# Four units instead of three go feature tile by feature tile at the start of a two-layer trunk

## The chip, the cores and the metric

The kernel runs on one core of a Trainium2 chip. The metric is the device time of one execution in microseconds (us). TensorE multiplies, VectorE (DVE) and ScalarE (ACT) read its results out of PSUM and work on them, GpSimd (POOL) helps with element-wise work, and SyncE (SP) issues the transfers (DMA) between HBM and the on-chip memory SBUF.

## What is computed

Two layers of a transformer trunk work on 640 tokens of 1024 features: 512 latent tokens and 128 context tokens. Cut to what matters here:

```python
def layer(x, cond, lp, layer_idx, ctx_cache):
    mod = silu(cond) @ lp["w_ada"] + lp["b_ada"]          # 6 * 1024 columns
    sh1, sc1, g1, sh2, sc2, g2 = split(mod, 6)
    y, new_ctx = mixers(x * (1.0 + sc1) + sh1, lp, ...)   # the input h of the projection
    x = layer_norm(ALPHA * x + g1 * y, ...)
    ...
def mixers(h, lp, lam, lam_init, ctx_cache):
    a_x, a_b, a_c, d_q, d_k, d_v, m_cq, m_ckv, m_kpe = split(h @ lp["w_in"])
    y_a = a_b * short_conv(a_c * a_x, lp["conv_w"])
    ...                                                   # differential attention on d_*, latent attention on m_*
```

The first layer can't start its projection h @ w_in before the columns sh1 and sc1 of mod are there, which takes 8.4 MB of w_ada.

## The kernel before

Features lie on the 128 partitions, tokens in the free dimension: h is 8 feature tiles (NK = 8) of 128 x 640, each held as a rounded part and a remainder (hi, lo), and so is every weight tile. One product is three matmuls: hi by hi, hi by lo, lo by hi. The 640 tokens are split into region A (columns 0 to 384) and region B (384 to 640), since one PSUM bank holds 512 columns. A unit is 128 output columns of w_in: 8 feature tiles x 2 regions x 3 = 48 matmuls. The units come in the order of WIN: ax0, ac0, ab0, ax1, dk0, dq0, dk1, dq1, dv, and so on. ax, ac and ab belong to the short convolution, dk and dq to the differential attention. dv has another shape (dv_job).

Startup. setup issues, on SP's one queue, w_ada in five groups (FIRST: feature tile 0, then 1 and 2, 3 and 4, 5 and 6, 7), after each group the x of its feature tiles, and then weight tiles of w_in up to the count in PUMP. ada_first multiplies a group of w_ada on TensorE (L461), transposes the sums (L468), and modulate makes h of these feature tiles (L631, L638, L639). jobs3 holds the matmuls of the first three units (L386), feature tile by feature tile, so that they can go on while later groups arrive. Each of the three has a PSUM tile of its own. The units after that go through job and matmul3 (L343), one unit after the other, region A for all feature tiles and then region B.

Weights. A weight tile arrives in one of three staging buffers (stg), ScalarE casts it to hi (L142) and VectorE subtracts to get lo (L144) into one of four buffers (wu). W.get hands out the next unit, W.done gives its buffer back, and pump starts what has become possible.

PSUM. In the stage "any", mm() hands out three tiles of two banks each in turn. From dq1 on (SCORE_AT) the stage is "score": two tiles and one for scores, in the same six banks. A tile is free again when what it held has been read: in_evac does that for each unit, ax by a copy on ScalarE (L854), ac by three products on VectorE (L865, L866, L868), ab by products on VectorE that read PSUM at the end of the convolution (L884 to L888), dk and dq by ScalarE (L905, L906, L918, L919).

After each unit that doesn't go through jobs3, self.ada(ADA_IN) adds one step of the modulation that later stages need: 16 small matmuls (L434) on tiles rawt of w_ada, an addition on VectorE (L497), and after four steps a transpose (L441). During dv the first scores (L1192) of the differential attention are made, from dqp and dkp, which dq0 and dk0 reach through HBM (ddq, ddk).

The order of the instructions on each engine is set when the program is built, by a planner that simulates the timeline; an edge (issue_after, the helper behind) can force one instruction behind another. On the chip each engine works through its list in that order.

Of the kernel before, what the change touches and what calls it, by code (L numbers as in the profile page):

```python
# [18 lines left out]
NK = 8  # L19
# [8 lines left out]
SKEW = 4  # L28
# [18 lines left out]
SPLIT_POOL = ("y3", "y4", "y7")  # L47
W_POOL = False
FIRST = ((0, 1), (1, 2), (3, 2), (5, 2), (7, 1))
PUMP = (3, 3, 3, 3, 4, 4)  # L50
MODV = True
PIN = 3
TABLE = True
# [41 lines left out]
REG = {"A": (0, 384), "B": (384, 640)}  # L95
# [97 lines left out]
class Trunk:  # L193
# [181 lines left out]
    def window(self, hooks):  # L375
        self.nhook, self.hooks, self.urgent = 0, hooks, None

    def jobs3(self, us, x):

        nc = self.nc  # L380
        out = [self.mm()[:, 128:768] for _ in us]
        for k in range(NK):
            for u, ps in zip(us, out):
                for c0, c1 in REG.values():
                    for i, (pw, px) in enumerate(((0, 0), (0, 1), (1, 0))):
                        nc.tensor.matmul(ps[:, c0:c1], u[:, pw, 128 * k:128 * k + 128], x(k, px)[:, c0:c1],  # L386
                                         start=(k == 0 and i == 0), stop=(k == NK - 1 and i == 2))
        return out


# [456 lines left out]
    def in_evac(self, l, n, ps, regs):  # L847
        nc = self.nc
        if n in ("ax0", "ax1"):
            if "B" in regs:  # L850
                self.ax = self.t(name="ax")
                self.axs[n] = self.ax
            c0, c1 = (0, T) if regs == "AB" else REG[regs]
            nc.scalar.copy(self.axs[n][:, c0:c1], ps[:, c0:c1])  # L854
        elif n in ("ac0", "ac1"):
            m = n[-1]
            if "B" in regs:
                u = self.t(name="upad", n=644)
                self.us[m] = u
                nc.vector.memset(u[:, 0:1], 0.0)  # L860
                nc.vector.memset(u[:, 513:515], 0.0)
                nc.vector.memset(u[:, 643:644], 0.0)
            u, ax = self.us[m], self.axs["ax" + m]
            if "A" in regs:
                nc.vector.tensor_mul(u[:, 1:257], ps[:, 0:256], ax[:, 0:256])  # L865
                nc.vector.tensor_mul(u[:, 515:643], ps[:, 256:384], ax[:, 256:384])  # L866
            if "B" in regs:
                nc.vector.tensor_mul(u[:, 257:513], ps[:, 384:640], ax[:, 384:640])  # L868
        elif n in ("ab0", "ab1"):
            m = int(n[-1])  # L870
            u = self.us[n[-1]]
            if "B" in regs:
                self.ys[m] = self.t(name="y")
                self.abt = self.t(name="abt")
            if regs != "AB":
                c0, c1 = REG[regs]
                nc.scalar.copy(self.abt[:, c0:c1], ps[:, c0:c1])
                if regs == "B":
                    return
                ps = self.abt  # L880
            y = self.ys[m]
            w = [self.col("conv_w", l, 2 * i + m) for i in range(3)]
            cv = self.t(name="cv", n=642)
            nc.gpsimd.tensor_scalar(cv, u[:, 0:642], w[0], 0.0, ALU.mult, ALU.add)  # L884
            nc.vector.scalar_tensor_tensor(cv, u[:, 1:643], w[1], cv, ALU.mult, ALU.add)
            nc.vector.scalar_tensor_tensor(cv, u[:, 2:644], w[2], cv, ALU.mult, ALU.add)
            nc.vector.tensor_mul(lat(y), lat(ps), two(cv[:, 0:512]))
            nc.vector.tensor_mul(y[:, 256:384], ps[:, 256:384], cv[:, 514:642])  # L888
            nc.sync.dma_start(self.yd[m], self.ys.pop(m))
        elif n[:3] == "ckv" or n[:2] == "cq":  # L890
            raw, sq = self.t(name="raw"), self.t(name="sqr")
            nc.scalar.copy(raw, ps)
            nc.scalar.activation(sq, raw, AF.Square)
            rows = self.raws.setdefault(n[:-1], [])
            if rows:
                (nc.vector if n in ("ckv1", "cq2") else nc.gpsimd).tensor_add(sq, sq, rows[-1][1])
            rows.append((raw, sq))
            if n == "ckv1":
                self.norm_ckv(l)
            elif n == "cq2":  # L900
                self.norm_cq(l)
        elif n[:2] == "dk":
            m = int(n[-1])
            src = self.t(name="dk")
            nc.scalar.copy(src, ps)  # L905
            nc.scalar.copy(self.kp32[:, m, :], ps[:, 256:384])  # L906
            self.rope_lat(src, nc.vector if "k" in ROPE_V else nc.gpsimd)
            nc.vector.tensor_copy(src[:, 256:384], self.ckT[:, m, :])

            def rest():  # L910
                self.dkh[m] = self.split(src, "dk")

            self.soon(DEFER[2], rest)
            nc.sync.dma_start(self.o["state_diff_k"][l, m], self.kp32[:, m, :])
        elif n[:2] == "dq":
            m = int(n[-1])
            src = self.t(name="dq")
            nc.scalar.activation(src, ps, AF.Copy, scale=DIFF_SCALE)  # L918
            nc.scalar.copy(self.qp32[:, m, :], src[:, 256:384])  # L919
            self.rope_lat(src, nc.vector if "q" in ROPE_V else nc.gpsimd)  # L920

            def rest():
                qh, ql = self.split_q(src, "dq")
                kh, kl = self.dkh.pop(m)
                for i, (q, k) in enumerate(((qh, kh), (qh, kl), (ql, kh))):
                    self.move(self.ddq[m][:, i, :], q)
                    self.move(self.ddk[m][:, i, :], k)
                if m == 0:
                    self.assemble_diff(0)

            self.soon(DEFER[2], rest)
# [104 lines left out]
    def stage_in(self, l):  # L1036
        nc, a = self.nc, self.a
# [17 lines left out]

        names = [n for n, _ in WIN]
        h = lambda k, p: self.h[k][p]
        nskew = SKEW if l else 3
        if not l:
            us = [self.W.get((n, l)) for n in names[:nskew]]  # L1060
            for n, ps in zip(names, self.jobs3(us, h)):
                self.W.done()
                self.in_evac(l, n, ps, "AB")
                self.tick()
        else:
            us = [self.W.get((n, l)) for n in names[:nskew]]
            for regs in "BA":
                if regs == "B":
                    self.window(NEXT_IN)
                for i in range(0, nskew, 2):  # L1070
                    for n, ps in zip(names[i:i + 2], self.jobs2(us[i:i + 2], h, regs, NK)):
                        self.in_evac(l, n, ps, regs)
                        if regs == "A":
                            self.W.done()
                            self.tick()
                self.ln_inputs()
            self.ln_outputs(0 if OUTR else 1 << 30)
        for n in names[nskew:]:
# [4 lines left out]
            else:  # L1083
                u = self.W.get((n, l))
                mid, end = STEPS.get(n, (0, 0))
# [625 lines left out]
```

## Time and profile before

| | us |
|---|---|
| median of 3 runs | 1777.19 |
| lowest and highest | 1774.91, 1778.72 |
| profiled execution | 1775.88 |
| its span, first to last instruction | 1774.1 |
| TensorE busy in the span | 1702.8 |

The profiled execution is one of its own, 1.31 us below the median. Its span leaves out what lies before the first and behind the last instruction, 1.8 us. In the profile, PE is TensorE's matmuls and PEld its weight loads, which overlap them; a matmul's end is modelled, so that bars of neighbouring matmuls overlap, and the distance of two starts says more than a bar's length. Times are counted from the start of the span.

### The profile page before, as it was taken

Reading aid. Unit: us, or ns where it says so; the run is one execution under the profiler, and the core shown is the slowest. Engines: PE = TensorE matmul, PEld = TensorE weight load, DVE = VectorE, ACT = ScalarE, POOL = GpSimd, SP = SyncE. Lnnn points to the kernel's source line nnn. Section 1 sums busy time; section 2 is a strip of 40 time slices with the busy share of each in tenths; the row PEclk is TensorE's granted clock in tenths of the full one; section 3 lists DMA queues with packets and bytes.
Section 4 is the critical chain, followed back from the end, with each engine's and each line's share of the span. In section 5 each row is a group of like instructions: output and inputs, shape, how many; then the busy total and the mean of one; then the engine's idle time right before and its main releaser. Section 6 shows DMA issues by size and latency. Waiting matters only on the chain. (4 is left out here: it accounts for less than half of the span.)

```text
span 1774.1 us, 29684 instructions
## 1 busy us (share of the span) xinstructions
PE 1702.8 (96%) x11983; PEld 1593.7 (90%) x11983; DVE 1021.1 (58%) x1824; ACT 590.6 (33%) x1010; POOL 420.0 (24%) x400
## 2 busy tenths in 40 slices
PE   8999989998999999999999899899989999999997
PEld 6998867698999999999989798677989999999997
DVE  3656776759566566856397558764682332232236
ACT  1334545525321121122243436554442212211221
POOL 0011113447701010110377111233582000000014
PEclk9999989999999999999989899899999999999998
DMA  9564584321355444544314544722122222222211
GB/s 333 196 204 140 168 250 145 109 90 48 101 149 150 149 136 140 174 130 150 93 51 166 170 113 149 210 64 84 48 75 81 72 75 81 64 79 84 68 53 59
DMA packets 100872, 217.38 MB, mean 123 GB/s; under 512 B 12160, under 2 KB 28928, under 8 KB 100736
## 3 DMA queue, kind: packets, MB, share of 16 engines
q1 hardware_dynamic: 100736, 215.50, 39.3%
q8 instruction: 94, 1.54, 0.4%
q14 instruction: 42, 0.34, 0.1%
HBM read 185.28 MB, written 30.18 MB: 121 GB/s over the span
## 5 line engine op out<-in xcount | busy, mean ns | idle before, releaser
L343 PE MATMUL mm<-h,wu 128*128 128x384 f32 (+1 forms) x4944 | 735.9, 310 | 0.2
L343 PEld LDWEIGHTS mm<-h,wu 128*128 128x128 f32 x4944 | 724.9, 189 | 6.9 <-issue 5.3
L142 ACT CAST wu<-stg 128x1024 fp32r<-128x1024 f32 (+2 forms) x200 | 201.5, 1011 | 701.3 <-issue 347.1
L144 DVE TENSOR_TENSOR wu<-stg,wu 128x1024 fp32r<-128x1024 f32 (+2 forms) x200 | 246.0, 1234 | 145.6 <-ACT wu L142 143.9
L343 PE MATMUL mm<-gh,wu 128*128 128x256 f32 (+1 forms) x1184 | 258.8, 310 | 0.0
L343 PEld LDWEIGHTS mm<-gh,wu 128*128 128x128 f32 x1184 | 198.7, 188 | 0.9 <-issue 0.6
L343 PE MATMUL mm<-gl,wu 128*128 128x384 f32 (+1 forms) x592 | 182.8, 309 | 0.0
L1196 DVE TENSOR_REDUCE nm<-mm 128x1 f32<-128x640 f32 x128 | 104.7, 818 | 54.7 <-PE mm L1192 53.8
L1545 DVE TENSOR_TENSOR gs<-gs,mm 128x640 f32<-128x640 f32 (+2 forms) x48 | 36.6, 763 | 152.7 <-PE mm L343 147.6
L653 DVE SCALAR_TENSOR_TENSOR x<-mm,ga,x 128x512 f32<-128x512 f32 x48 | 35.9, 749 | 146.2 <-PE mm L343 146.2
L672 POOL TENSOR_TENSOR accS<-x 128x640 f32<-128x640 f32 x4 | 10.0, 2490 | 443.6 <-DVE x L659 418.5
L343 PEld LDWEIGHTS mm<-gl,wu 128*128 128x128 f32 x592 | 111.4, 188 | 0.2 <-issue 0.2
L512 DVE SCALAR_TENSOR_TENSOR acc<-rawt,scT,acc 128x512 f32<-128x512 f32 x98 | 75.8, 773 | 57.8 <-DMA rawt<-in_w_ada 56.1
L364 PE MATMUL mm<-h,wu 128*128 128x384 f32 (+1 forms) x576 | 95.6, 329 | 1.0 <-DVE v L694 0.5
L364 PEld LDWEIGHTS mm<-h,wu 128*128 128x128 f32 x576 | 91.5, 206 | 3.3 <-issue 0.8
L343 PE MATMUL mm<-hi,wu 128*128 128x384 f32 (+1 forms) x400 | 89.8, 311 | 0.1
L510 POOL TENSOR_SCALAR acc<-rawt,scT 128x512 f32<-128x512 f32 x14 | 9.8, 701 | 313.0 <-PE tr L527 312.9
L1192 PE MATMUL mm<-mk,mq 96*128 96x384 f32 (+1 forms) x384 | 75.3, 337 | 5.8 <-ACT P L1207 2.3
L517 DVE SCALAR_TENSOR_TENSOR rawt<-rawt,scT 128x512 f32<-128x512 f32 x98 | 74.7, 763 | 2.1 <-POOL rawt L510 2.1
L1192 PEld LDWEIGHTS mm<-mk,mq 96*128 96x128 f32 x384 | 64.1, 201 | 12.7 <-ACT P L1207 4.9
L343 PEld LDWEIGHTS mm<-hi,wu 128*128 128x128 f32 x400 | 68.0, 188 | 2.6 <-issue 1.5
L1207 ACT ACTIVATE P<-mm,nm 128x640 f32<-128x640 f32 x56 | 44.6, 797 | 57.3 <-DVE nm L1196 45.0
(279 smaller groups left out, 2446.8 us busy)
## 6 DMA issues: line engine op xcount, KB each, us to landing
stg<-in_w_ff SPq DMA_DIRECT2D x104, 512.0 KB, 3.6
rawt<-in_w_ada SPq DMA_DIRECT2D x160, 256.0 KB, 3.0
stg<-in_w_in SPq DMA_DIRECT2D x30, 512.0 KB, 4.4
stg<-in_w_ff SPq DMA_DIRECT2D x32, 448.0 KB, 3.3
raw<-in_w_ada SPq DMA_DIRECT2D x32, 256.0 KB, 6.2
stg<-in_w_out SPq DMA_DIRECT2D x16, 512.0 KB, 4.3
mk<-kd SPq DMA_DIRECT2D x32, 240.0 KB, 5.8
mq<-qd SPq DMA_DIRECT2D x32, 192.0 KB, 5.5
```

The lines of the kernel that those rows point to most:

```text
L142: nc.scalar.copy(u[:, 0, :ncol], t[:, :ncol])
L144: (nc.gpsimd if self.lo_pool else nc.vector).tensor_sub(u[:, 1, :ncol], t[:, :ncol], u[:, 0, :ncol].bitcast(F32))
L343: self.last = nc.tensor.matmul(out, w(k, pw), x(k, px), start=(k == 0 and i == 0), stop=(k == nk - 1 and i == 2)).ins
L364: self.last = nc.tensor.matmul(ps[:, c0:c1], u[:, pw, 128 * k:128 * k + 128], x(k, px)[:, c0:c1], start=(k == 0 and i == 0), stop=(k == nk ...
L512: nc.vector.scalar_tensor_tensor(self.acc[0], w, c[0], self.acc[0], ALU.mult, ALU.add)
L517: nc.vector.scalar_tensor_tensor(self.acc[1], w, c[1], self.acc[1], ALU.mult, ALU.add)
L653: nc.vector.scalar_tensor_tensor(lat(x), lat(ps), ga[:, 0, s, m:m + 1], lat(x), ALU.mult, ALU.add)
L672: nc.gpsimd.tensor_add(self.accS[:, c0:c1], self.first[0][:, c0:c1], x[:, c0:c1])
L1192: nc.tensor.matmul(ps[:, 128 + c0:128 + c1], q[:96, qc:qc + 128], k[:96, c0:c1], start=(i == 0), stop=(i == len(pairs) - 1))
L1196: nc.vector.tensor_reduce(nm, s, axis=AX.X, op=ALU.max, negate=True)
L1207: self.exp_end = nc.scalar.activation(P, s, AF.Exp, bias=nm, accum_out=sm).ins
L1545: nc.vector.tensor_mul(gs[:, c0:c1], gs[:, c0:c1], ps[:, c0:c1])
```

## The change

jobs4 takes the place of jobs3: four units (ax0, ac0, ab0, ax1) go feature tile by feature tile. They share three PSUM tiles: the first holds region A of ax0 and of ac0 in a bank each, the second region A of ab0 and of ax1, the third region B of all four, two units to a bank. In a shared bank only the first unit's first matmul carries start, and the second unit's first is put behind it (opened). On the last feature tile the order is forced: region B of ax0 and ac0, region A of both, then the same for ab0 and ax1. in_evac takes the two pieces one by one; ab is copied to abt by ScalarE first, as in the second layer. PUMP lets the fourth weight tile go out after the second group of w_ada and the fifth after the last. ax1 is no longer followed by a call of ada.

```diff
--- before.py
+++ after.py
@@ -47,7 +47,7 @@
 SPLIT_POOL = ("y3", "y4", "y7")
 W_POOL = False
 FIRST = ((0, 1), (1, 2), (3, 2), (5, 2), (7, 1))
-PUMP = (3, 3, 3, 3, 4, 4)
+PUMP = (3, 4, 4, 4, 5, 5)
 MODV = True
 PIN = 3
 TABLE = True
@@ -375,16 +375,31 @@
     def window(self, hooks):
         self.nhook, self.hooks, self.urgent = 0, hooks, None
 
-    def jobs3(self, us, x):
-
-        nc = self.nc
-        out = [self.mm()[:, 128:768] for _ in us]
+    def jobs4(self, us, x):
+
+
+
+        nc = self.nc
+        t = [self.mm() for _ in range(3)]
+        out = []
+        for j in range(4):
+            b = 512 * (j // 2) + 256 * (j % 2)
+            out.append([(0, 384, t[j // 2][:, 512 * (j % 2):512 * (j % 2) + 384]), (384, 640, t[2][:, b:b + 256])])
+        every = [(j, r) for j in range(4) for r in range(2)]
+        ends = [(0, 1), (1, 1), (0, 0), (1, 0), (2, 1), (3, 1), (2, 0), (3, 0)]
+        ins = opened = None
         for k in range(NK):
-            for u, ps in zip(us, out):
-                for c0, c1 in REG.values():
-                    for i, (pw, px) in enumerate(((0, 0), (0, 1), (1, 0))):
-                        nc.tensor.matmul(ps[:, c0:c1], u[:, pw, 128 * k:128 * k + 128], x(k, px)[:, c0:c1],
-                                         start=(k == 0 and i == 0), stop=(k == NK - 1 and i == 2))
+            end = k == NK - 1
+            for j, r in ends if end else every:
+                c0, c1, ps = out[j][r]
+                first, second = r == 1 and j % 2 == 0, r == 1 and j % 2 == 1
+                for i, (pw, px) in enumerate(((0, 0), (0, 1), (1, 0))):
+                    new = k == 0 and i == 0
+                    with self.behind(opened if new and second else ins if end else None):
+                        ins = nc.tensor.matmul(ps, us[j][:, pw, 128 * k:128 * k + 128], x(k, px)[:, c0:c1],
+                                               start=new and not second, stop=end and i == 2 and not first).ins
+                    if new and first:
+                        opened = ins
         return out
 
 
@@ -851,7 +866,8 @@
                 self.ax = self.t(name="ax")
                 self.axs[n] = self.ax
             c0, c1 = (0, T) if regs == "AB" else REG[regs]
-            nc.scalar.copy(self.axs[n][:, c0:c1], ps[:, c0:c1])
+            for c0, c1, p in ps if isinstance(ps, list) else [(c0, c1, ps[:, c0:c1])]:
+                nc.scalar.copy(self.axs[n][:, c0:c1], p)
         elif n in ("ac0", "ac1"):
             m = n[-1]
             if "B" in regs:
@@ -861,20 +877,22 @@
                 nc.vector.memset(u[:, 513:515], 0.0)
                 nc.vector.memset(u[:, 643:644], 0.0)
             u, ax = self.us[m], self.axs["ax" + m]
+            psA, psB = [p for _, _, p in ps] if isinstance(ps, list) else (ps[:, 0:384], ps[:, 384:640])
+            if "B" in regs:
+                nc.vector.tensor_mul(u[:, 257:513], psB, ax[:, 384:640])
             if "A" in regs:
-                nc.vector.tensor_mul(u[:, 1:257], ps[:, 0:256], ax[:, 0:256])
-                nc.vector.tensor_mul(u[:, 515:643], ps[:, 256:384], ax[:, 256:384])
-            if "B" in regs:
-                nc.vector.tensor_mul(u[:, 257:513], ps[:, 384:640], ax[:, 384:640])
+                nc.vector.tensor_mul(u[:, 1:257], psA[:, 0:256], ax[:, 0:256])
+                nc.vector.tensor_mul(u[:, 515:643], psA[:, 256:384], ax[:, 256:384])
         elif n in ("ab0", "ab1"):
             m = int(n[-1])
             u = self.us[n[-1]]
             if "B" in regs:
                 self.ys[m] = self.t(name="y")
                 self.abt = self.t(name="abt")
-            if regs != "AB":
-                c0, c1 = REG[regs]
-                nc.scalar.copy(self.abt[:, c0:c1], ps[:, c0:c1])
+            if regs != "AB" or isinstance(ps, list):
+                c0, c1 = REG[regs[0]]
+                for c0, c1, p in ps if isinstance(ps, list) else [(c0, c1, ps[:, c0:c1])]:
+                    nc.scalar.copy(self.abt[:, c0:c1], p)
                 if regs == "B":
                     return
                 ps = self.abt
@@ -1055,10 +1073,10 @@
 
         names = [n for n, _ in WIN]
         h = lambda k, p: self.h[k][p]
-        nskew = SKEW if l else 3
+        nskew = SKEW
         if not l:
             us = [self.W.get((n, l)) for n in names[:nskew]]
-            for n, ps in zip(names, self.jobs3(us, h)):
+            for n, ps in zip(names, self.jobs4(us, h)):
                 self.W.done()
                 self.in_evac(l, n, ps, "AB")
                 self.tick()
```

## Rows read from the trace of the kernel before

**Rows 1.** Page, busy time of the engines: us (share of the span) xinstructions.

```profile
PE 1702.8 (96%) x11983; PEld 1593.7 (90%) x11983; DVE 1021.1 (58%) x1824; ACT 590.6 (33%) x1010; POOL 420.0 (24%) x400
```

**Rows 2.** Busy us by stretch (xinstructions), then granted clock, DMA share, GB/s.

```profile
13.00:25.00 12.00, 11.25 (x99) 8.35 (x99) 5.58 (x14) 1.56 (x4) 0.00 (x0) 0.73 1.09 366
25.00:36.00 11.00, 10.90 (x105) 8.74 (x107) 3.53 (x14) 1.18 (x4) 0.00 (x0) 1.00 1.09 361
36.00:46.00 10.00, 10.00 (x93) 8.37 (x90) 3.83 (x14) 1.64 (x4) 0.00 (x0) 1.00 1.06 347
46.00:58.00 12.00, 11.83 (x97) 10.66 (x95) 8.00 (x32) 5.81 (x10) 0.00 (x0) 1.00 0.48 164
```

**Rows 3.** Groups of TensorE's instructions by form, 25.1 to 57.5 us.

```profile
L386 PE MATMUL mm<-h,wu 128*128 128x384 f32 x63 | 16.0, 356 | 0.8 <-ACT h L638 0.8
L386 PE MATMUL mm<-h,wu 128*128 128x256 f32 x63 | 11.4, 284 | 0.0
L461 PE MATMUL ac<-raw,scT 128*32 128x128 f32 x144 | 11.1, 276 | 0.0
```

**Rows 4.** Timeline of TensorE: start, us, engine, line, what, [idle before]; startup.

```profile
25.10 0.79 PE L386 MATMUL mm<-h,wu 128*128 128x384 f32 x3 [0.85 <-ACT h L638]
...
34.91 1.94 PE L461 MATMUL ac<-raw,scT 128*32 128x128 f32 x32
...
45.13 3.27 PE L461 MATMUL ac<-raw,scT 128*32 128x128 f32 x32
48.33 2.19 PE L386 MATMUL mm<-h,wu 128*128 128x384 f32 x12
...
57.41 0.42 PE L434 MATMUL tr<-rawt,scT 128*32 128x128 f32 x8
...
58.78 14.27 PE L343 MATMUL mm<-h,wu 128*128 128x384 f32 x96
```

**Rows 5.** Timeline of TensorE, the first scores.

```profile
103.19 0.46 PE L1192 MATMUL mm<-dkp,dqp 96*128 96x384 f32 x2
103.49 5.37 PE L992 MATMUL mm<-wu,h 128*128 128x288 f32 x39
```

**Rows 6.** Timeline of ScalarE.

```profile
57.09 1.05 ACT L142 CAST wu<-stg 128x1024 fp32r<-128x1024 f32 x1 [3.73 <-issue]
58.04 0.69 ACT L854 COPY ax<-mm 128x640 f32<-128x640 f32 x1
...
89.00 0.69 ACT L905 COPY dk<-mm 128x640 f32<-128x640 f32 x1
89.59 0.27 ACT L906 COPY kp<-mm 128x128 f32<-128x128 f32 x1
```

**Rows 7.** Timeline of VectorE, behind the first three units.

```profile
58.17 1.23 DVE L144 TENSOR_TENSOR wu<-stg,wu 128x1024 fp32r<-128x1024 f32 x1
59.31 0.42 DVE L865 TENSOR_TENSOR upad<-mm,ax 128x256 f32<-128x256 f32 x1
```

**Rows 8.** Tile raw, 32.9 to 33.9 us: its last load, and time to landing.

```profile
L182 SPq DMA_DIRECT2D raw<-in_w_ada x1: 967/967/967, 32.9 to 32.9; - x1
...
DMA to landing us min/median/max: 7.1/7.1/7.1
```

**Rows 9.** Busy us by stretch: from dk1's last matmul to dq1's first.

```profile
88.30:92.90 4.60, 2.43 (x51) 1.25 (x50) 1.50 (x5) 1.43 (x3) 0.00 (x0) 1.00 0.83 267
```

**Rows 10.** Timeline of TensorE, the same place in the second layer.

```profile
943.56 28.16 PE L343 MATMUL mm<-h,wu 128*128 128x384 f32 x192
...
982.19 0.87 PE L1192 MATMUL mm<-dkp,dqp 96*128 96x384 f32 x2 [7.28 <-DMA dkp<-ddk]
982.86 6.58 PE L992 MATMUL mm<-wu,h 128*128 128x288 f32 x39
```

**Rows 11.** Tile dkp, 90.25 to 90.72 us: its first load, and time to landing.

```profile
L273 SPq DMA_DIRECT2D dkp<-ddk x1: 412/412/412, 90.3 to 90.3; - x1
...
DMA to landing us min/median/max: 4.6/4.6/4.6
```

## The prediction

> **What bounds the kernel now.** I read the page first, then tables of busy time by stretch, then the timeline engine by engine for the first 105 us, then the same place in the second layer. TensorE is busy 1702.8 us, 96% of the span [rows 1], so a change pays only where TensorE stands still. The change touches the start, where the loads of w_ada run at about 360 GB/s, and there the reader must not stop at the DMA column. From 25 us on TensorE is busy 10.90 of 11, 10.00 of 10 and 11.83 of 12 us [rows 2], at full clock. Real standstill before 58.78 is small: one wait of 0.85 us at 25.10 [rows 4], and the half-speed stretch inside 13 to 25, where the granted clock averages 0.73 [rows 2].
>
> Matmul bars overlap, so I checked by counting. Between 25.10 and 57.41 there are 126 matmuls of the projection (L386) and 144 of the modulation (L461) [rows 3]. Of the latter, the last 32 took 3.20 us (from 45.13 to 48.33), the others about 61 ns each, as 32 of them in 1.94 us show [rows 4]; together 10.0 us of the 32.3. That leaves 22.3 us for the 126 matmuls, three transposes, eight ada products and some twenty changes from one kind to the other. Unbroken, projection matmuls run 192 in 28.16 us, 147 ns each [rows 10], so the 126 need 18.5 us. At most 3.8 us is hidden room, and the transposes, the products and the changes of kind take most of it. TensorE, not the DMA, sets the pace from 25 us on. The loads are ahead: the last piece of w_ada is issued at 32.9 and lands 7.1 us later, at 40.0 [rows 8], and TensorE multiplies it only in the run that starts at 45.13 [rows 4].
>
> **The change, part by part.**
> *Work moved.* The unit ax1 (48 matmuls, 14.27 us for two units, so 7.1 us [rows 4]) moves from behind 58.78 into the startup. As TensorE is full there, it pushes everything after it back by nearly what it saves later. What it can fill is the wait of 0.85 us, by the six matmuls of the first feature tile (6 x 147 ns = 0.9 us), if ax1's weights are split by then, and some of the 3.8 us. Bounds 0 and 4.7 us; I take half of the wait, 0.4 us, since the 3.8 us have their takers.
> *Loads moved.* The fourth weight tile now goes out behind the second group of x instead of behind the last one: 0.52 MB at 361 GB/s [rows 2], 1.45 us, ahead of three groups of w_ada. The last piece has 5 us or more in hand (40.0 against 45.13), so this costs nothing there; if a load of the third group is met on arrival, at most 1.45 us. The fifth tile takes the fourth's old place; it is behind all that the startup waits for. Its cover is the same 5 us.
> *The end of the four units.* All four weight buffers are now held until the end, while before ax1 stood ready as a fourth unit and covered what dk0 needs. dk0 needs two things. Its weight tile: ax0's last matmul is the ninth of the last 24, so its buffer is free 15 x 147 ns = 2.2 us before the end; then a cast of 1.05 us on ScalarE [rows 6] and a subtract of 1.23 us on VectorE [rows 7]. And its PSUM tile, which now holds region A of ax0 and of ac0: ax0's copy (0.69 us whole [rows 6], about 0.9 in two pieces), then the three products of ac0 (two of 0.42 us [rows 7] and one half as wide, about 1.1 us). Both chains share the two engines: 1.05 + 0.9 + 1.1 and some 0.4 us for three hand-overs is 3.45 us against 2.2 us, so dk0 starts about 1.3 us after the last matmul. Before, the same place took 1.37 us, from 57.41 to 58.78, for a cast in front of ax0's copy [rows 6], with two sets of ada products inside (0.42 us for the one at 57.41 [rows 4]); those fit into the new gap as well. So the old gap goes and a new one of equal size comes: -0.1 us. Its bounds: 0.9 us (the ada products alone) and 2.6 us (if the subtract of a second unit is set before ac0's products).
> *Evacuation.* ab0 is copied by ScalarE into abt in two pieces (0.9 us more) instead of being read from PSUM by VectorE, and ax0 and ax1 take two copies each. All of it lies beside dk0's 7.1 us of matmuls, in which ScalarE and VectorE have about 6 and 8 us to do; a microsecond of VectorE's may run into dk0's rotary steps, and nobody waits for those before the first scores.
> *Ring of PSUM tiles.* This is the part with a price. Three tiles go round. Before, ax0, ac0, ab0, ax1, dk0, dq0, dk1 take 0, 1, 2, 0, 1, 2, 0, and when the stage "score" opens a new pool, dq1 takes the first place again: dk1's. So dq1 waits for dk1's two reads by ScalarE, 89.00 to 89.86 [rows 6], behind a cast, and the planner set three ada steps into that wait. TensorE is busy 2.43 of the 4.60 us from 88.30 to 92.90 [rows 9]: the ada steps, back to back, wait for each other's additions and for rawt. After, four units take only three tiles, dk0, dq0, dk1 take 0, 1, 2, and dq1 finds dk0's place, read long ago. The second layer has that order already (eight half units, then 2, 0, 1, and dq1 on dq0's place), and its dk0 to dq1 run as 192 matmuls without a break [rows 10]. The ada work stays, spread between the units. Gain 4.60 - 2.43 = 2.2 us; bounds 0 (the ada steps wait as long elsewhere) and 2.2.
> *Counts.* One call of ada falls away in this stage, so every ada step moves one place back; the total is unchanged, and the steps lie beside matmuls. I cost it at 0, with 1 us to either side, since the planner sets the attention anew.
>
> Sum: -0.4 - 0.1 - 2.2 = -2.7 us on an execution of 1775.88 us (span 1774.1 and 1.8 around it), that is 1773.2. The median of the runs is 1.31 us above this execution, so the forecast is 1777.19 - 2.7 = **1774.5 us**.
>
> **The rivals.**
> 1. *The startup has room.* Weight loads are busy 8.74, 8.37 and 10.66 of 33 us [rows 2], so 5.2 us are not loads. If ax1 slips into these, the gain is 2.7 + 5.2 = 7.9 us: 1769.3. Against it: the modulation's loads are of 32 columns and shorter than its products, and the count above leaves at most 3.8 us, most of it taken. The Trainium skill ("Trainium Kernel Development and Optimization", Performance Expectations) takes this rival's side: it calls matmul busy time a bad measure, because matmuls are pipelined, and weight-load busy time a good one. The trace so far leaves that open.
> 2. *The ring gives nothing.* If dq1 waits for something else than dk1's place, or the ada steps wait as long in the new gap, only -0.5 us is left: 1776.7. For it: of the 2.2 us idle, part is a wait for rawt, which would also be met elsewhere.
> 3. *The first scores come too early: slower.* Pair 0's keys are issued at 90.3 and land 4.6 us later, at 94.9 [rows 11]; the scores start at 103.19 [rows 5]. dq0 ends at 80.5 (two units of 7.1 us and one set of ada products after 65.9), so the way from there to the landing takes 14.4 us. After, dq0 to the first scores is two units, two ada steps and a tile of dv: 14.3 + 0.8 + 3.4 = 18.5 us. It decides when that way takes over 18.5 us. In the second layer it does: dq0 ends near 957.6 (half of the 28.16 us after 943.56), the keys come at 982.19, 24.5 us, and TensorE waits 7.28 us [rows 10]. At that length it would wait 6.0 us here, and after it the next 39 matmuls of dv took 6.58 us there [rows 10] against 5.37 here [rows 5], 1.2 us more: 6.0 + 1.2 - 2.7 = +4.5, 1781.7. Against it: VectorE has no layer norm to do in this stretch.
> 4. *ax1's weights hold TensorE.* It works in order; if the planner puts ax1's first matmuls before the second modulation group, TensorE stands from about 19.5 to 24.0: 4.5 us, less the 0.8 us that the wait at 25.10 gives back: 1777.19 - 2.3 + 3.7 = 1778.6.
>
> **How the numbers follow.** Forecast 0.46, rival 1 0.16, rival 2 0.19, rival 3 0.09, rival 4 0.10. A measurement of this kernel tells about 0.2% (3.6 us) from no change. The forecast's own range is 1772 to 1777, a third of it below 1773.6. Faster: 0.16 + 0.16 = 0.32. Slower by over 0.2%: rival 3 and a little of rival 4, with the attention's new order on top, 0.14. The rest, 0.54, is within. The range reaches from rival 1 to just short of rival 3: 1769 to 1781.
>
> **What would show it.** Right: dk0's first matmul near 65.4 us, TensorE full from 25 us to the end of the four units, one gap of 1.3 us there, and dq1 behind dk1 without a gap. Wrong: dk0 before 62 us (there was room), a wait of the first scores for dkp, a gap before 25 us for ax1's weights, or gaps around the ada steps in other places.

## The result and the profile after

The changed kernel takes 1789.95 us (median; 1789.46 to 1793.39), the kernel before beside it 1776.97 us (1774.91 to 1778.72). The ratio is 1.008, interval 1.0067 to 1.0093: 13 us slower, where 2.7 us faster was forecast and the range ended at 1781.

Page of the changed kernel, busy time of TensorE in us (share of the span) and instructions; its span is 1791.5 us:

```profile
PE 1712.2 (96%) x11983; PEld 1601.6 (89%) x11983; DVE 1021.8 (57%) x1824; ACT 591.2 (33%) x1014; POOL 416.3 (23%) x400
```

The work is the same as in [rows 1], yet TensorE's bars sum to 9.4 us more and the span is 17.4 us longer. So there are new waits, and stretches at the lower clock. The first place to look is the one that was changed.

Busy us of the changed kernel by stretch, then granted clock, DMA share and GB/s:

```profile
13.00:25.00 12.00, 11.44 (x99) 8.70 (x99) 5.21 (x12) 1.77 (x4) 0.00 (x0) 0.72 1.08 373
25.00:36.00 11.00, 9.44 (x84) 7.74 (x79) 4.74 (x12) 2.59 (x5) 0.00 (x0) 0.84 1.08 367
36.00:46.00 10.00, 10.00 (x101) 8.23 (x100) 4.27 (x15) 1.64 (x4) 0.00 (x0) 1.00 1.01 316
46.00:58.00 12.00, 12.00 (x92) 11.36 (x91) 6.80 (x30) 3.76 (x8) 0.00 (x0) 1.00 0.40 150
...
88.30:97.50 9.20, 4.97 (x66) 2.88 (x66) 3.99 (x12) 1.43 (x3) 0.00 (x0) 0.73 0.98 297
```

TensorE is full from 36 us to the end of the four units, as in [rows 2]. The granted clock of 0.84 behind 25 us is not the change's: a second profile of the same kernel has 1.00 there and starts dk0 3.3 us earlier (below). But the stretch from dk1's last matmul to dq1's first, 4.60 us in [rows 9], is 7.7 us long now (from 89.05 to 96.79 in the timeline below), and 6.7 us in the second profile.

Timeline of TensorE, changed kernel (start, us, engine, line, what, idle before it and who ended it); L399 is the four units, L449 and L456 are ada steps:

```profile
56.02 10.29 PE L399 MATMUL mm<-h,wu 128*128 128x256 f32 x69
66.24 0.64 PE L449 MATMUL tr<-rawt,scT 128*32 128x128 f32 x16
67.09 3.21 PE L343 MATMUL mm<-h,wu 128*128 128x384 f32 x17 [0.21 <-DVE upad L885]
...
89.05 0.64 PE L449 MATMUL tr<-rawt,scT 128*32 128x128 f32 x16
90.11 0.65 PE L449 MATMUL tr<-rawt,scT 128*32 128x128 f32 x16 [0.41 <-DVE ada_acc L512]
91.17 0.33 PE L456 MATMUL tr<-first,ada_acc 128*128 128x128 f32 x1 [0.41 <-DVE ada_acc L512]
93.83 1.31 PE L449 MATMUL tr<-rawt,scT 128*32 128x128 f32 x16 [2.34 <-DMA rawt<-in_w_ada]
96.20 0.66 PE L449 MATMUL tr<-rawt,scT 128*32 128x128 f32 x8 [1.06 <-DVE sh L841]
96.79 8.42 PE L343 MATMUL mm<-h,wu 128*128 128x384 f32 x48
```

Two things are to be seen. dq1 no longer waits for ScalarE's reads of dk1 (the runs with an edge, below, show it), and still the planner set the ada steps between dk1 and dq1, one behind the other, each waiting for its addition or its load (2.34 us for rawt). And dq1's 48 matmuls start and end 8.42 us apart instead of some 7.3: the clock had fallen. That explains a few microseconds, not 13.

For the rest I took the starts of a few landmarks in every profile. The first row is the kernel before in us from the span's start, the others are differences to it. "FF" is the first matmul (L343) of the first layer's feed-forward behind its first four units, which go two by two; "latent" are the first scores of the latent attention. The kernels of the other rows follow in the next section; "pinned" are those with no ada step between dk1 and dq1. A profiled execution lies up to 3.4 us from its kernel's median, and the clock of the startup alone moves a whole row by 3 us or more, so the steps from column to column say more than a column.

| kernel | dk0 | dv | projection's last matmul | latent | FF | dv, layer 2 | latent, layer 2 | span |
|---|---|---|---|---|---|---|---|---|
| before | 65.89 | 100.00 | 184.5 | 246.8 | 453.9 | 971.6 | 1120.6 | 1774.1 |
| changed | +1.20 | +5.05 | +4.68 | +8.48 | +12.12 | +12.11 | +16.18 | +17.41 |
| changed, again | -2.12 | +1.05 | +0.67 | +5.20 | +8.78 | +8.72 | +13.86 | +16.13 |
| changed, 13 calls | -2.24 | +0.70 | +0.77 | +0.84 | +1.32 | +1.41 | +0.76 | +2.30 |
| before, 12 calls | -1.48 | -0.46 | -0.78 | +2.11 | +6.92 | +7.12 | +6.16 | +6.96 |
| before, 14 calls | -0.73 | -0.96 | -1.41 | +1.09 | +5.45 | +6.26 | +5.61 | +5.39 |
| changed, call before out | -2.17 | +1.86 | +1.50 | +5.47 | +7.08 | +7.95 | +8.63 | +7.90 |
| changed, pinned | -1.91 | -6.50 | -5.61 | -0.98 | +1.96 | +1.73 | +4.75 | +5.00 |
| changed, 13, pinned | -2.26 | -6.06 | -1.05 | +0.42 | +0.60 | +0.58 | +0.57 | +0.98 |
| before, pinned | +0.01 | -2.31 | +1.66 | +1.66 | +2.38 | +2.35 | +2.44 | +2.23 |
| changed, pinned, call before out | -3.82 | -8.39 | -7.49 | -2.17 | -0.99 | -0.81 | -1.52 | -1.51 |
| changed, ckv0's call behind ab1 | -1.89 | -5.70 | -7.00 | -2.24 | -4.31 | -4.45 | -0.13 | +1.25 |
| before, the same | -0.86 | -3.18 | -4.49 | +4.64 | +2.11 | +2.12 | +1.36 | +0.93 |
| changed, ckv0's call behind cq1 | -1.48 | -5.28 | -4.84 | -0.40 | -3.06 | -3.08 | -3.97 | -2.46 |
| changed, ckv0's call behind ckv1 | -2.12 | -5.92 | -5.87 | -2.29 | -2.78 | -2.28 | -2.81 | -1.89 |
| before, ckv0's call behind cq1 | +0.18 | -2.14 | -2.43 | +3.14 | +0.52 | +0.87 | +0.39 | -0.17 |

Read the row "changed, again": the projection that was changed ends 0.7 us late. Then 4.5 us are lost on the way to the latent scores, 3.6 more up to the feed-forward, nothing in it, and 7.4 in the second layer. None of these places holds an edited line. What reaches them is the one call of ada that fell away: all steps behind it come one place later.

### The profile page after: what moved, and what is told of

Read it like the earlier page. It is cut to its first block, busy times and chain, and to the rows that moved or that the text cites. A ratio compares the mean times of both kernels' runs of the same rounds, so it can differ in the third digit from the quotient of the medians.

```text
span 1791.5 us, 29671 instructions
## 1 busy us (share of the span) xinstructions
PE 1712.2 (96%) x11983; PEld 1601.6 (89%) x11983; DVE 1021.8 (57%) x1824; ACT 591.2 (33%) x1014; POOL 416.3 (23%) x400
## 5 line engine op out<-in xcount | busy, mean ns | idle before, releaser
L343 PE MATMUL mm<-h,wu 128*128 128x384 f32 (+1 forms) x4896 | 730.1, 310 | 0.3 <-DVE upad L885 0.2
L343 PEld LDWEIGHTS mm<-h,wu 128*128 128x128 f32 x4896 | 719.3, 189 | 6.8 <-issue 4.9
L343 PE MATMUL mm<-gh,wu 128*128 128x256 f32 (+1 forms) x1184 | 258.1, 309 | 0.0
L343 PEld LDWEIGHTS mm<-gh,wu 128*128 128x128 f32 x1184 | 198.6, 188 | 0.6 <-issue 0.6
L343 PE MATMUL mm<-gl,wu 128*128 128x384 f32 (+1 forms) x592 | 182.7, 309 | 0.0
L343 PEld LDWEIGHTS mm<-gl,wu 128*128 128x128 f32 x592 | 111.3, 188 | 0.2 <-issue 0.2
L343 PE MATMUL mm<-hi,wu 128*128 128x384 f32 (+1 forms) x400 | 90.9, 314 | 1.2 <-ACT mqs L1178 0.7
L343 PEld LDWEIGHTS mm<-hi,wu 128*128 128x128 f32 x400 | 68.6, 190 | 4.7 <-issue 1.5
L343 PE MATMUL mm<-lo,wu 128*128 128x384 f32 (+1 forms) x200 | 62.2, 311 | 0.0
```

The costliest lines, as they stand in the source:

```text
L343: self.last = nc.tensor.matmul(out, w(k, pw), x(k, px), start=(k == 0 and i == 0), stop=(k == nk - 1 and i == 2)).ins
```

## The experiments

None of these kernels leaves out work; they place calls of ada, each of which emits the next step of a fixed list. "13 calls" are those of the first layer's projection in the kernel before; the change has 12.

**The changed kernel again**, for a second profile.

> The changed kernel once more, for a second profile. Both theories: about 1790 us, 13 us over before, with the same offsets in the first layer: dv begins 5 us later than before, the first latent-attention scores 8.5 us, the feed-forward part 12 us. What differs between its two profiles is not the change's.

1791.03 us, ratio 1.0066 (1.0044 to 1.0088). The loss is there in both profiles, and so is the order of the instructions.

**The missing call given back.** If the loss is in the count, this takes it away and leaves the rest of the change.

```diff
                 self.tick()
+            self.ada(ADA_IN)
         else:
```

> The changed kernel with one call of ada put back behind the four units, so that 13 calls fall into the first projection as before. Theory 1 (two separate losses: 5 us up to dv from the startup's tail and from the ada steps in front of dq1, and about 8 us behind it because every later ada step moved one place and the planner set the work anew): dv still 5 us late, nothing added behind it, 1782 us. Theory 2 (the later loss comes from the shifted start itself, whatever the count of calls): 13 us as in the changed kernel, 1790 us.

1777.49 us, ratio 1.0003 (0.9992 to 1.0014). Neither expectation came true: dv is 0.7 us late and not 5, and the time is below both. One line gives back 12.5 to 13.5 us: with the call, all of the loss is gone. What is left of the change is worth nothing that can be measured, and not the 2.7 us of the forecast either.

**The count alone**: the kernel before, without the call behind ax1.

```diff
-            self.ada(ADA_IN)
+            self.ada(ADA_IN if l or n != "ax1" else 0)
```

> The kernel before without the call of ada behind ax1: 12 calls in the first projection, the startup untouched. Theory 1: dv at its old time within 1 us, then up to 8 us lost behind it, 1785 us. Theory 2: no difference beyond 1 us, 1777 us.

1783.53 us, ratio 1.0037 (1.0025 to 1.0049). About 7 us, with nothing else changed, as the first expectation had it. Its profile shows two places. From the projection's end to the latent scores 2.9 us are lost: 80 small products of ada stand there instead of 64 (3.4 us of TensorE's time instead of 2.6), and TensorE's waits sum to 7.4 us instead of 6.0, with one of 0.9 us for rv and one of 0.7 us for mqs that are new. The next 4.8 us are lost nearly all at the end of the out projection. There VectorE has to finish the sums accS and accQ, which TensorE needs for the norm. VectorE in the kernel before, the steps of ada (L512, L517) among the sums (L676):

```profile
392.61 1.20 DVE L512 SCALAR_TENSOR_TENSOR acc<-rawt,scT,acc 128x512 f32<-128x512 f32 x1 [2.99 <-DMA rawt<-in_w_ada]
393.74 1.22 DVE L517 SCALAR_TENSOR_TENSOR rawt<-rawt,scT 128x512 f32<-128x512 f32 x1
...
395.46 0.43 DVE L676 TENSOR_TENSOR accS<-accS,x 128x256 f32<-128x256 f32 x1
...
396.76 0.42 DVE L676 TENSOR_TENSOR accS<-accS,x 128x256 f32<-128x256 f32 x1
```

The same in the kernel before with 12 calls:

```profile
394.31 1.22 DVE L512 SCALAR_TENSOR_TENSOR acc<-rawt,scT,acc 128x512 f32<-128x512 f32 x1 [2.33 <-DMA rawt<-in_w_ada]
395.46 0.74 DVE L517 SCALAR_TENSOR_TENSOR rawt<-rawt,scT 128x512 f32<-128x512 f32 x1
396.12 0.74 DVE L512 SCALAR_TENSOR_TENSOR acc<-rawt,scT,acc 128x512 f32<-128x512 f32 x1
396.78 0.74 DVE L517 SCALAR_TENSOR_TENSOR rawt<-rawt,scT 128x512 f32<-128x512 f32 x1
...
398.96 0.75 DVE L512 SCALAR_TENSOR_TENSOR acc<-rawt,scT,acc 128x512 f32<-128x512 f32 x1 [0.51 <-DMA rawt<-in_w_ada]
399.62 0.75 DVE L517 SCALAR_TENSOR_TENSOR rawt<-rawt,scT 128x512 f32<-128x512 f32 x1
...
401.14 0.43 DVE L676 TENSOR_TENSOR accS<-accS,x 128x256 f32<-128x256 f32 x1
```

From 390 us on, six operations of ada instead of two stand in front of the last sum, and TensorE waits for it. Timeline of TensorE in the kernel before with 12 calls:

```profile
401.71 0.35 PE L685 MATMUL mm<-first,accS 128*128 128x2 f32 x2 [2.44 <-DVE accS L676]
```

The wait is 2.44 us. The same place in the kernel before, where it is 0.47 us:

```profile
397.33 0.35 PE L685 MATMUL mm<-first,accS 128*128 128x2 f32 x2 [0.47 <-DVE accS L676]
```

Behind the wait, busy us by stretch, with the granted clock at 0.51 for 7 us in the kernel before with 12 calls:

```profile
402.00:409.00 7.00, 6.86 (x24) 6.83 (x24) 2.79 (x15) 0.39 (x1) 0.40 (x1) 0.51 0.01 2
```

and at 1.00 in the kernel before:

```profile
397.50:404.50 7.00, 5.47 (x35) 5.09 (x35) 4.86 (x18) 1.48 (x3) 1.96 (x2) 1.00 0.01 4
```

The changed kernel has the same six operations and a wait of 2.32 us.

**The call given back later**, ahead of the out projection, so that the attention keeps the late steps and all behind it has those of before.

```diff
+        if not l and not s:
+            self.ada(ADA_IN)
         for m in range(n0):
```

> The changed kernel with its missing call of ada given back later: one call ahead of the first output tile of the out projection of layer 1, so that the out projection and all behind it hold the same ada steps as before, while the projection, the first layer's attention and the startup stay as in the changed kernel. If the loss is in the count of steps and in two places: the attention's 4 us stay, the 3 us between it and the first feed-forward go, the second layer goes back to its old order, and the time is about 1776.5 + 4 = 1780.5 (1779 to 1783). If the loss is in the attention alone, or in the second layer for a reason that isn't the count: 1787 to 1791.

1781.61 us, ratio 1.0034 (1.0022 to 1.0047), as expected. The wait for accS is down to 0.64 us, the way from the latent scores to the feed-forward costs 1.6 us instead of 3.6, and all that follows 0.8 instead of 7.4; the attention's 4 us stay.

**One call more** in the kernel before. Does each step that comes earlier bring something, or does any other count cost?

```diff
-            self.ada(ADA_IN)
+            self.ada(ADA_IN if l or n != "ax1" else 2 * ADA_IN)
```

> The kernel before with one more call of ada behind ax1, fourteen instead of thirteen, so that every later ada step comes one place earlier. If the price is one of position (each step that slides into the attention and the out projection costs TensorE and VectorE time there), one step fewer there gives back 1 to 3 us: 1774 to 1776. Rival, every other count of steps disturbs an order that suits thirteen: 1780 to 1785, about as much as with twelve.

1781.84 us, ratio 1.0031 (1.002 to 1.0043): the rival. With 14 calls the loss comes from the latent scores to the feed-forward (+1.09 to +5.45), where one wait of 3.17 us for PT is new. So it isn't that late steps are dear: with the rest of the program as it is, 13 calls are better than either neighbour.

**No ada step between dk1 and dq1.** An edge puts the steps that stood there behind dq1's last matmul. First in the changed kernel with its 12 calls (ada_pin starts as None; "..." marks a cut).

```diff
-        self.ada_products(ps, key, 2 * q, 2 * q + 2)
+        with self.behind(self.ada_pin):
+            self.ada_products(ps, key, 2 * q, 2 * q + 2)
...
-            self.ada(ADA_IN)
+            if n == "dq1" and not l:
+                self.ada_pin = self.last
+            self.ada({"dk1": 0, "dq1": 2 * ADA_IN}.get(n, ADA_IN))
```

> The changed kernel with the ada steps from the third on forced behind dq1's last matmul. Theory 1: TensorE goes from dk1 to dq1 without a gap, no half clock there, dv begins 5 to 6 us earlier than in the changed kernel (near 99 us), and the loss behind dv stays: 1784 us. Rival: the steps wait as long at the place they are moved to, or the first scores wait for dkp: 1790 us.

1781.26 us, ratio 1.0032 (1.0021 to 1.0043). dv comes 7.5 us earlier than in the second profile without the edge. Behind it the losses are of the same kind as without it: 4.6 us in the attention, 2.9 up to the feed-forward, 3.3 in the second layer. Still the time is 8.7 to 9.8 us below the changed kernel's, and below both expectations, with the same 12 calls. So the call isn't the only way to get the loss back: setting two of the steps elsewhere does most of it, too.

**The same with 13 calls, and in the kernel before**: what is the PSUM place itself worth?

> The changed kernel with the thirteenth call of ada behind the four units, and with two ada steps taken from between dk1 and dq1 and set behind dq1's last matmul, so that nothing stands between dk1 and dq1. If the shared bank's free PSUM place is worth what the prediction gave it, and only the planner's ada steps stood in the way: dq1's first matmul within 0.5 us of dk1's last, no half-clock stretch inside dq1, the first matmul of dv 6 us earlier than with the thirteenth call alone, and the time 1777.5 - 6 = 1771.5 us (1770 to 1773). Rival, the steps only wait elsewhere: dv early, but the lead is gone by the first latent scores, 1776 to 1778.

> The kernel before, with the same two ada steps set behind dq1's last matmul and nothing else changed. dq1 still waits for ScalarE's second read of dk1. If the PSUM place is what counts: a gap of 1.5 to 2 us stays between dk1 and dq1, and the time is 1776.5 - 3 = 1773.5 us, 2 us above the changed kernel with thirteen calls and the same order. Rival, the ada steps between dk1 and dq1 are all of it, and the place nothing: the same gain as there, about 1771.5.

Changed kernel: 1776.19 us, ratio 1.0 (0.999 to 1.001), which is its rival. Kernel before: 1777.42 us, ratio 1.0004 (0.9994 to 1.0014), which misses both expectations. The intervals overlap, so the place's worth doesn't show in the time. Timeline of TensorE in the kernel before with the edge:

```profile
85.75 2.64 PE L343 MATMUL mm<-h,wu 128*128 128x256 f32 x21
89.92 7.27 PE L343 MATMUL mm<-h,wu 128*128 128x384 f32 x48 [1.52 <-ACT kp L907]
```

And in the changed kernel with 13 calls and the edge:

```profile
83.80 9.64 PE L343 MATMUL mm<-h,wu 128*128 128x256 f32 x69
```

That is the prediction's wait, uncovered: without ada steps in it, dq1 waits 1.52 us for the second read of dk1 in the kernel before, and not at all in the changed one, where dk1 and dq1 are one row. The lead of 6.06 us at dv is 1.05 at the projection's end. Timeline of TensorE in the changed kernel with 13 calls and the edge, where it goes:

```profile
139.27 0.64 PE L449 MATMUL tr<-rawt,scT 128*32 128x128 f32 x16
139.84 0.56 PE L1214 MATMUL mm<-dkp,dqp 96*128 96x384 f32 x2
140.71 0.33 PE L456 MATMUL tr<-first,ada_acc 128*128 128x128 f32 x1 [0.31 <-DVE ada_acc L513]
142.42 0.56 PE L1214 MATMUL mm<-dkp,dqp 96*128 96x384 f32 x2 [1.38 <-ACT Pt L1229]
142.91 0.74 PE L449 MATMUL tr<-rawt,scT 128*32 128x128 f32 x16
144.33 1.33 PE L829 MATMUL mm<-first,ny 128*128 128x128 f32 x5 [0.68 <-DVE ny L335]
145.31 6.86 PE L343 MATMUL mm<-h,wu 128*128 128x384 f32 x26
```

Waits of 1.38 and 0.68 us follow each other, and then 26 matmuls take 6.86 us, where they take 4.67 in the pinned kernel with 12 calls. Busy us by stretch of the same kernel:

```profile
143.30:150.20 6.90, 6.22 (x32) 5.87 (x21) 6.55 (x16) 1.93 (x4) 1.36 (x1) 0.51 0.93 267
```

**One more call moved away from there**: the one behind ckv0 goes behind ab1, in both kernels (`"ckv0": 0, "ab1": 2 * ADA_IN` added to the dictionary above).

> The changed kernel with thirteen calls and with no ada step between dk1 and dq1, as in the run with these two, and with one call more moved: the one behind ckv0 goes behind ab1, so that the sum of the calls is again thirteen. In the run without this the lead of 6.1 us at dv fell to 4.7 us at ckv0 and 1.0 at the end of the projection: an ada step and its subtract stood between the scores and the norm's row near 142 us, TensorE waited 1.4 and 0.7 us there and fell to a granted clock of 0.5 from 143.3 to 150.1. If that place is where the lead goes: no half clock there, the end of the projection 5 us ahead of the kernel before instead of 1, 3 to 5 us of it left at the first latent scores, and the time 1772 to 1774 us. Rival, the lead has no taker because the attention that follows is bound by VectorE and ScalarE, or its steps are planned anew and lose as much: the lead is gone by 247 us and the time 1776 to 1782.

> The kernel before with the same three moves of ada calls, and none of the change. Its dq1 still waits 1.5 us for ScalarE's second read of dk1. If the calls' places are all that counts: the same gain as in the changed kernel with them, less 1.5 to 2.5 us for that wait and for the startup, 1774 to 1776. If the change's own part is worth nothing at the end: the same time as that kernel, within 1 us.

Changed kernel: 1778.69 us, ratio 1.0014 (1.0005 to 1.0023). Kernel before: 1775.86 us, ratio 1.0001 (0.9992 to 1.001). So the changed kernel's rival came true, and the kernel before comes out 2.8 us below it, which neither of its expectations had, though its time lies in the range of the first. In the changed kernel the half clock is gone, the projection ends 7.00 us ahead, and 4.45 us of that reach the second layer. There they are lost within some 150 us, up to the latent scores. Timeline of TensorE in that kernel, second layer:

```profile
1097.22 0.66 PE L1289 MATMUL tr<-first,P 128*128 128x128 f32 x4 [0.38 <-ACT PT L267]
...
1099.58 1.05 PE L1289 MATMUL tr<-first,P 128*128 128x128 f32 x4 [1.12 <-DVE PT L269]
```

These waits, and one of 1.31 us for ny at 1023, are not in the kernel before (its transposes of P idle 0.1 us in all there). In this stretch 572 of TensorE's matmuls (from 1021 to 1110 us in the kernel before) stand in another order than in the kernel before; the last 4345 have one order in all kernels (the two with the call before out have a third order in part of the stretch). Of all kernels here three have this other order: the changed one, the pinned one with 12 calls, and this one. Just these lose 3.0 to 5.1 us between dv and the latent scores of the second layer; all others lie between a loss of 0.7 and a gain of 1.0. What makes the planner take it isn't the count alone, since this kernel has 13; that stays open.

**The pin and the late call together**, with the changed kernel's 12 calls.

> The changed kernel with its twelve calls, with no ada step between dk1 and dq1, and with the missing call given back ahead of the out projection of layer 1. The two edits were run apart: the first brought the first latent scores 1.0 us ahead of the kernel before, the second took the loss from there to the first feed-forward from 2.7 to 0.5 us and that of the second layer from 7.4 to 0.8 us. If these add: -1.1 + 0.5 + 0.8, so 1776.5 to 1777 us. Rival, the planner's order isn't a sum of places: 1779 to 1783.

1776.01 us, ratio 1.0005 (0.9994 to 1.0016): the places add up as expected, within the noise.

**Two other places for ckv0's call** that leave the order from the out projection on as in the kernel before, and the first of them in the kernel before (`"ckv0": 0` with `"cq1": 2` or `"ckv1": 2`).

> The changed kernel with thirteen calls, none between dk1 and dq1, and the one behind ckv0 set behind cq1 instead of ab1. With it behind ab1 the kernel was 7.0 us ahead of the kernel before at the end of layer 1's projection and still 4.3 us ahead at the second layer's projection, and lost 5 us there, where its order of instructions was another than in the kernel before. Here the order of instructions from the out projection of layer 1 to the end is that of the kernel before. If the change's lead is real and was lost only to that other order: 2 to 4 us ahead from the first feed-forward to the end, 1772.5 to 1774.5 us. Rival, the attention of layer 1 eats the lead because its waits for ScalarE and for loads don't move: within 1 us of the kernel before at the first feed-forward, 1776 to 1777.

> The same with the call of ckv0 set behind ckv1, a third place. The order from the out projection on is again that of the kernel before. If only the order from there on decides, the same as with it behind cq1, within 1 us. If the steps' places inside the projection and the attention decide: a difference of 2 us or more that is there already at the first latent scores.

> The kernel before with the same moves of ada calls as the run with the call behind cq1, and none of the change; its order from the out projection on is that of the kernel before, too. dq1 waits 1.5 us for ScalarE's second read of dk1. If the change is worth its 1.5 us there and 0.7 us at the startup: 2 us more than the changed kernel with these moves, 1774.5 to 1776.5. If its worth doesn't reach the end: the same time within 1 us.

Behind cq1: 1773.57 us, ratio 0.9982 (0.9973 to 0.999). Behind ckv1: 1773.79 us, ratio 0.998 (0.9971 to 0.9988). The kernel before with cq1: 1773.98 us, ratio 0.9982 (0.9973 to 0.9991). All three are faster than both kernels, 3.2 to 3.6 us below the kernel before, and the one without the change does as well as those with it. The times of the first two are as expected; of the third, the second expectation came true. By the profiles the change is 3.1 us ahead at dv and 2.3 at the end, but the profiled execution of the kernel before with cq1 is the slowest of its 11 (1775.7 us). By the medians 0.4 us are left. The means of the 11 runs of each lie 0.2 us apart, with 0.7 us to either side, so no gain shows, and one of 2 us is ruled out. What is worth 3 us here is where the ada steps stand.

Timeline of TensorE in the changed kernel with cq1: from dk0 to the first scores nothing is left that waits.

```profile
64.41 1.82 PE L343 MATMUL mm<-h,wu 128*128 128x384 f32 x9 [0.20 <-DVE upad L886]
...
83.70 10.52 PE L343 MATMUL mm<-h,wu 128*128 128x384 f32 x75
...
98.14 0.46 PE L1214 MATMUL mm<-dkp,dqp 96*128 96x384 f32 x2
```

## Why the prediction was wrong, point by point

*Counts* is the step that failed. The prediction put the call that falls away at 0, "with 1 us to either side, since the planner sets the attention anew". It measured 13 us: the changed kernel with and without it, 1789.95 or 1791.03 against 1777.49. By itself, in the kernel before, it costs 7 us: from a projection that ends 0.8 us early, 2.9 in the attention and 4.8 from there to the feed-forward, nearly all at the end of the out projection. In the changed kernel the second layer's other order comes on top, with 4 to 5 us up to the latent scores. The prediction did say that every step moves one place back, and then followed the steps only up to the attention. It should have gone to each later stage that takes ada steps at fixed places and asked which step stands there now, and who waits on that engine. At the out projection one pair of ada's operations stands in front of the sums in the kernel before, and three pairs with the steps one place later.

*Ring of PSUM tiles* was right in mechanism and wrong in worth. The wait for dk1's reads was there, 1.52 us when uncovered, and the change removes it. But the 2.2 us were to come because "the ada work stays, spread between the units". It wasn't spread. That is rival 2 in its own words, the ada steps wait as long in the new gap, and its time, 1776.7, fits the 1777.49 (1773.48 to 1781.18) with 13 calls. That it fits so well is partly luck: by the profile dk0 starts 2.2 us ahead there, not 0.5, and dq1 takes 2.3 us more than in the kernel before, since the clock is down for it, which the rival left out.

*Work moved* and *the end of the four units* came close. At nearly the same clock from 13 to 25 us (0.76 against 0.73) dk0 starts at 64.41 in the changed kernel with cq1 instead of 65.89, 1.5 us earlier, where 0.5 was forecast. But not by filling the wait of 0.85 us, as the forecast had it: that wait stands as before, and one of 0.70 us is new behind it. Timeline of TensorE in the changed kernel with cq1:

```profile
24.92 0.45 PE L399 MATMUL mm<-h,wu 128*128 128x384 f32 x1 [0.85 <-ACT h L654]
26.06 1.14 PE L399 MATMUL mm<-h,wu 128*128 128x384 f32 x5 [0.70 <-DVE h L655]
```

So about 1 us must come from matmuls that follow each other closer behind it, out of the 3.8 us that the forecast left to others; no run takes that apart. (The prediction's list of standstills also leaves out 2.0 us in front of the projection's first matmul, at 12.89; the changed kernel waits there, too.) In the changed kernel the gap behind the four units is 0.85 us, not 1.3, and 16 ada products fill 0.64 of it. ScalarE, then VectorE in the changed kernel:

```profile
64.10 1.05 ACT L142 CAST wu<-stg 128x1024 fp32r<-128x1024 f32 x1 [5.91 <-issue]
65.06 0.47 ACT L870 COPY ax<-mm 128x384 f32<-128x384 f32 x1
```

```profile
65.19 1.23 DVE L144 TENSOR_TENSOR wu<-stg,wu 128x1024 fp32r<-128x1024 f32 x1 [6.35 <-ACT wu L142]
66.33 0.42 DVE L884 TENSOR_TENSOR upad<-mm,ax 128x256 f32<-128x256 f32 x1
66.67 0.28 DVE L885 TENSOR_TENSOR upad<-mm,ax 128x128 f32<-128x128 f32 x1
```

The cast starts 2.2 us before the units end, as worked out. But the chain is shorter than the 3.45 us of the forecast: the copy of ax0 runs beside the subtract, and only two of ac0's products (0.42 and 0.28 us) read the tile that dk0 takes, 3.0 us in all. So rival 1 had a little for it, about 1 us of room and not 5.2. The Trainium skill ("Trainium Kernel Development and Optimization", Performance Expectations) would read headroom from the weight loads; from 25 to 36 us they rose from 0.79 of the time [rows 2] to between 0.83 (with cq1) and 0.89 (9.80 of 11 us in the last row of this document) in the profiles of the change at full clock there, so the trace agrees in sign, with less of a gain.

*Loads moved* and *evacuation* were free, as predicted: no wait for a weight tile in the startup, none for a PSUM tile behind dk0. So rival 4 is out. Rival 3 is out too: in the changed kernel with cq1 dq0 ends at 79.4, the first load of dkp is issued at 89.1 and lands 3.1 us later, 12.8 us behind dq0's end where 18.5 us was the limit, and the scores start at 98.14 without a wait.

## What to carry to other kernels

Where a program is set in order by a planner and side work is dealt out by calls, a change that drops one call moves all side work behind it; cost it by looking at every later place where a step meets an engine that others wait for, and build the change with the count kept before judging the rest. A wait removed in front of a filler is no gain as long as the filler stays in the same place. And a lead at one landmark is worth what is left of it at the next few: here 6 us at 100 us were 1 us at 185 and none at 247.

## What was unexpected of the hardware

A gap can cost more than its length. Behind the ada steps between dk1 and dq1, with TensorE busy 4.25 of 6.30 us, dq1's 48 matmuls took 9.58 us instead of 7.27. In the kernel before, the gap of 4.60 us at the same place, with TensorE busy 2.43 us of it and the granted clock at 1.00 [rows 9], had no such cost: there dq1 took 7.28 us. What makes the difference between the two is open. Timeline of TensorE, dq1 in the kernel before, then in the changed kernel with 13 calls:

```profile
92.89 7.28 PE L343 MATMUL mm<-h,wu 128*128 128x384 f32 x48
```

```profile
91.29 9.58 PE L343 MATMUL mm<-h,wu 128*128 128x384 f32 x48
```

Busy us by stretch of the changed kernel with 13 calls, the first with the end of dk1 in it:

```profile
85.00:91.30 6.30, 4.25 (x63) 2.58 (x61) 1.69 (x6) 1.43 (x3) 0.00 (x0) 0.86 0.83 265
91.30:100.87 9.57, 9.57 (x54) 9.57 (x51) 3.79 (x8) 0.73 (x1) 0.00 (x0) 0.74 1.03 291
```

And the startup isn't the same in each execution. The changed kernel started dk0 at 67.09 in one profile and at 63.77 in the other. The pinned kernel with the call before out, whose edits lie behind the startup, started it at 62.07, with a clock that did not fall. Busy us by stretch of that kernel:

```profile
13.00:25.00 12.00, 10.68 (x108) 7.75 (x110) 7.59 (x21) 3.74 (x7) 0.00 (x0) 1.00 1.08 372
25.00:36.00 11.00, 11.00 (x128) 9.80 (x128) 4.66 (x15) 1.64 (x4) 0.00 (x0) 1.00 1.08 370
```

In the first profile, with granted clocks of 0.72 and 0.84 in these stretches, dk0 starts 5 us later, as much as most of the effects here.
